# Every third weight slab: the low part made by an accumulating DMA instead of a VectorE subtraction

## The chip, the cores and the metric

The kernel runs on one core of a Trainium2 chip. The metric is device time in microseconds (us), of the whole kernel in one launch; the time of a kernel is the median of its runs. A profiled execution gives the rest: what each engine did at what time. The engines are TensorE (PE; its weight loads are listed as PEld), VectorE (DVE), ScalarE (ACT), GpSimd (POOL) and SyncE (SP, which here only issues DMAs).

## The reference

One layer of a gated recurrent block with an MLP, over 256 frames of width 2048, in float32:

```python
h = RMSNorm(x)
z = h @ w_in + b_in                      # 2048 -> 7 x 2048: xa ya cb cc cx ga gb
xa = rg_lru(causal_dwconv4(xa) + conv_a_b)   # gates by 8 blocks of 256, then a forward scan
out_a = (xa * gelu(ya)) @ w_pa
out_b = (cb * causal_dwconv3(cc * cx)) @ w_pb
x = x + (sigmoid(ga) * out_a + sigmoid(gb) * out_b) @ w_o
x = x + relu(RMSNorm(x) @ w_mlp1)**2 @ w_mlp2    # 2048 -> 8192 -> 2048
return RMSNorm(x)
```

The weights are some 312 MB of float32, each read once.

## The kernel before, in words

Activations lie transposed: features on the 128 partitions, the 256 frames along the free axis. A product is formed for 128 output features at a time, over 2048 input features (16 steps of 128), or 1024 to 4096 in some stages. So that float32 accuracy survives TensorE's faster fp32r format, every operand is split into two fp32r parts: a high part, the value rounded to fp32r, and a low part, the value minus the high part. A step of the product is two matmuls (in `product`, L232 and L233): the high weights times both parts of the activations (512 columns), and the low weights times the high part of the activations (256 columns).

The weights come in slabs of 128 x 1024 float32 (512 KB): 8 steps of one output tile. There are 596 of them, in the order in which TensorE will use them. The class `Weights` streams them. `make` takes the next slab and does three things with it:

- L61: SP issues the DMA that loads the slab into a tile `raw` (4 buffers);
- L63: ScalarE casts `raw` into `hi` (profile name `whi`, 4 buffers);
- L64: VectorE subtracts, `lo = raw - hi` (profile name `wlo`, 4 buffers).

`take` hands TensorE the next slab, after it has let `make` run up to three slabs ahead (`LOOK = 3`). Lines under `high_priority(AHEAD)` are ordered as if they stood 300 instructions earlier in the program, so that the split of a coming slab goes ahead of ScalarE's and VectorE's other work. A planner puts the instructions of each engine into one fixed order and inserts the waits: a buffer is filled again once its last reader is done, and each engine, as well as each queue of DMA issues, works in order. The first four slabs are made by two calls with `parts=4`, a quarter slab at a time, interleaved with the loads of x.

Beside the splits, ScalarE takes the second half of each product out of PSUM (`added`, L238; six PSUM buffers `psz`) and does the activations; VectorE adds, scales, convolves and scans. POOL does nothing but a few memsets: the zero edges of the convolution inputs `xa` (L289) and `cx` (L308), twice each in each of the eight groups of the first stage, which lasts to about 500 us. The stages follow one another in program order: eight groups of the input projection with convolutions, gates and scan; then per output tile the two merge gates and the projections of both branches; the product with `w_o`; and two halves of the MLP.

Of the kernel before, what the change touches and what calls it, by code (L numbers as in the profile page):

```python
# [9 lines left out]
F32 = mybir.dt.float32  # L10
F32R = mybir.dt.float32r
AF = mybir.ActivationFunctionType
ALU = mybir.AluOpType

P = 128
S = 256
# [6 lines left out]
EPS = 1e-6  # L23
LOOK = 3
AHEAD = 300
# [11 lines left out]


class Weights:
    """Streams [128, ncol] slabs of weights and splits each exactly into two fp32r parts."""  # L40

    def __init__(self, tc, raw_pool, hi_pool, lo_pool, slabs):
        self.tc, self.nc, self.slabs = tc, tc.nc, slabs
# [2 lines left out]
        self.at = 0  # L46

    def make(self, n=1, parts=1, before=None):
        """Loads and splits the next n slabs, in that many parts; before(i) precedes part i."""
        nc = self.nc  # L50
        w = HALF * P // parts
        got = [(self.slabs[len(self.made) + m],
                self.raw_pool.tile([P, HALF * P], F32, name="raw"),
                self.hi_pool.tile([P, HALF * P], F32R, name="whi"),
                self.lo_pool.tile([P, HALF * P], F32R, name="wlo")) for m in range(n)]
        for i in range(parts):
            c = slice(i * w, (i + 1) * w)
            if before is not None:
                before(i)
            for src, raw, hi, lo in got:  # L60
                nc.sync.dma_start(raw[:, c], src[:, c])  # L61
                with self.tc.high_priority(AHEAD):
                    nc.scalar.copy(hi[:, c], raw[:, c])  # L63
                    nc.vector.tensor_tensor(lo[:, c], raw[:, c], hi[:, c].bitcast(F32), ALU.subtract)  # L64
        self.made += [(hi, lo) for _, _, hi, lo in got]
# [3 lines left out]
            self.make()  # L69

    def first(self, n):
        """The first n slabs, which make() has made."""
        self.at = n
        return self.made[:n]

# [9 lines left out]
def trunk(ctx: ExitStack, tc: tile.TileContext, xT, par, w_in, w_lru, w_pa, w_pb, w_o, w_1, w_2, out):  # L85
    nc = tc.nc
# [9 lines left out]
    slabs = []  # L96
# [28 lines left out]
    x = keep.tile([P, NT, S], F32, name="x")  # L125
# [3 lines left out]
        return pr[:, OFF[name] + j:OFF[name] + j + 1]  # L129

    def split(dst, src):
        """dst [P, 2, S] fp32r <- src as two parts."""
        nc.scalar.copy(dst[:, 0, :], src)  # L133
        nc.vector.tensor_tensor(dst[:, 1, :], src, dst[:, 0, :].bitcast(F32), ALU.subtract)  # L134

# [12 lines left out]
    ssq = keep.tile([P, S], F32, name="ssq")  # L148

    def total(parts):  # L150
        """PSUM [P, S]: the sum over partitions and parts, on every partition."""
        ps = psl.tile([P, 512], F32, name="psl")
        for i, sq in enumerate(parts):
            nc.tensor.matmul(ps[:, :S], ones, sq, start=i == 0, stop=i == len(parts) - 1)  # L154
        return ps[:, :S]

    def rsqrt(dst, parts):
        """dst [P, S] <- 1 / sqrt(mean of the squares + EPS)."""
        ps = total(parts)
        y = wk.tile([P, S], F32, name="t")  # L160
        nc.scalar.activation(y, ps, AF.Sqrt, scale=1.0 / D, bias=eps)
        m = wk.tile([P, S], F32, name="low")
        nc.vector.tensor_scalar(m, ps, 1.0 / D, EPS, ALU.mult, ALU.add)
        nc.vector.reciprocal(y, y)
        nc.vector.tensor_tensor(m, m, y, ALU.mult)
        nc.vector.scalar_tensor_tensor(m, m, -0.5, y, ALU.mult, ALU.mult)
        nc.vector.scalar_tensor_tensor(dst, m, 1.5, y, ALU.add, ALU.mult)
# [14 lines left out]
    nc.sync.dma_start(pr[:, NT:], par[:, NT:])  # L182

    def squares(src, j):
        """ssq, by partition, of the tiles up to j."""
        if j == 0:
            nc.scalar.activation(ssq, src, AF.Square)
        else:
            sq = wk.tile([P, S], F32, name="s")
            nc.scalar.activation(sq, src, AF.Square)  # L190
            nc.vector.tensor_tensor(ssq, ssq, sq, ALU.add)

    lam = pr[:, OFF["lam"]:OFF["lam"] + NT]
    s4 = keep.tile([P, NT], F32, name="s4")
# [2 lines left out]
    s2 = keep.tile([P, NT], F32, name="s2")  # L197

    def decay():
        """s4 <- -4 softplus(-lam)."""  # L200
        nc.scalar.activation(s2, lam, AF.Abs)
        nc.scalar.activation(sg, s2, AF.Sigmoid, scale=-1.0)
        nc.vector.tensor_scalar(sd, sg, -1.0, 2.0, ALU.mult, ALU.add)
        nc.vector.reciprocal(sd, sd)
        nc.vector.tensor_tensor(sg, sg, sd, ALU.mult)
        nc.vector.tensor_tensor(s2, sg, sg, ALU.mult)
        nc.vector.tensor_scalar(sd, s2, 1.0 / 17, 1.0 / 15, ALU.mult, ALU.add)
        for n in (13, 11, 9, 7, 5, 3, 1):
            nc.vector.tensor_tensor(sd, sd, s2, ALU.mult)
            nc.vector.tensor_scalar(sd, sd, 1.0 / n, None, ALU.add)  # L210
        nc.vector.tensor_tensor(sd, sd, sg, ALU.mult)
        nc.vector.tensor_scalar(s2, lam, -1.0, 0.0, ALU.mult, ALU.max)
        nc.vector.scalar_tensor_tensor(s2, sd, 2.0, s2, ALU.mult, ALU.add)
        nc.vector.tensor_scalar(s4, s2, -4.0, None, ALU.mult)

    def product(acts, k0, nh, flat=False):
        """PSUM [P, 2, S]: the sum of its two halves, or if flat its first half, is the next weights' product
        with acts."""
        ps = psz.tile([P, 2, S], F32, name="psz")
        n = nh * HALF  # L220
        for c in range(nh):
            hi, lo = W.take()
            for k in range(HALF):
                a = acts(k0 + c * HALF + k)
                i = c * HALF + k
                if flat:
                    w = slice(k * P, (k + 1) * P)
                    nc.tensor.matmul(ps[:, 0, :], hi[:, w], a[:, 0, :], start=i == 0, stop=False)  # L228
                    nc.tensor.matmul(ps[:, 0, :], hi[:, w], a[:, 1, :], start=False, stop=False)  # L229
                    nc.tensor.matmul(ps[:, 0, :], lo[:, w], a[:, 0, :], start=False, stop=i == n - 1)  # L230
                    continue
                nc.tensor.matmul(ps, hi[:, k * P:(k + 1) * P], a, start=i == 0, stop=False)  # L232
                nc.tensor.matmul(ps[:, 1, :], lo[:, k * P:(k + 1) * P], a[:, 0, :], start=False, stop=i == n - 1)  # L233
        return ps
# [13 lines left out]
    def z_product():  # L248
        return product(lambda k: xg[:, k], 0, 2)
# [2 lines left out]
        z_done(z_product(), j, dst, func)  # L252

    def first_pair():
        """The products of the first two tiles, side by side, as x and the weights come in."""
        w = W.first(4)
        two = [psz.tile([P, 2, S], F32, name="psz") for _ in range(2)]
        for k in range(NT):
            for m in range(2):
                hi, lo = w[k // HALF * 2 + m]  # L260
                c = slice(k % HALF * P, (k % HALF + 1) * P)
                nc.tensor.matmul(two[m], hi[:, c], xg[:, k], start=k == 0, stop=False)  # L262
                nc.tensor.matmul(two[m][:, 1, :], lo[:, c], xg[:, k, 0, :], start=False, stop=k == NT - 1)  # L263
        return two
# [16 lines left out]
    with tc.tile_pool(name="w1", bufs=1) as w1:  # L281
        first_norm(w1)
        for g in range(NB):
# [3 lines left out]
            for m in range(2):  # L287
                j = 2 * g + m
# [17 lines left out]
            for m in range(2):  # L306
                j = 2 * g + m
# [9 lines left out]
            if g == 0:  # L317
                decay()
            hi, lo = W.take()
# [13 lines left out]
            r, i = gates  # L333
# [16 lines left out]
            for m in range(2):  # L350
                split(ua[:, 2 * g + m], v[:, m, :])
# [3 lines left out]
    for j in range(NT):  # L355
        sa = wk.tile([P, S], F32, name="s")
        sb = wk.tile([P, S], F32, name="s")
        z_tile(Z_GA + j, sa, AF.Sigmoid)
        z_tile(Z_GB + j, sb, AF.Sigmoid)
        tb = added(product(lambda k: ub[:, k], 0, 2))  # L360
        nc.vector.tensor_tensor(sb, sb, tb, ALU.mult)
        ta = added(product(lambda k: ua[:, k], 0, 2))
        nc.vector.tensor_tensor(sa, sa, ta, ALU.mult)
        nc.vector.tensor_tensor(sa, sa, sb, ALU.add)
        split(mg[:, j], sa)
# [8 lines left out]
    for h in range(2):  # L374
# [10 lines left out]
        for j in range(NT):  # L385
            flat = h == 1 and j == NT - 1
# [10 lines left out]
    nc.scalar.activation(last, x[:, NT - 1, :], AF.Square)  # L397
    nc.scalar.activation(x[:, NT - 1, :], x[:, NT - 1, :], AF.Copy, scale=pc("gf", NT - 1))
    rsqrt(rs, [ssq, last])
    at = 0  # L400
    for n in (3, 4, 4, 3, 1, 1):
# [4 lines left out]


def _slabs(w):
    """[K, N] -> [N / 128, K / 1024, 128, 1024]: per 128 columns and 1024 rows, one slab with the rows' low
    index on the partitions."""  # L410
    k, n = w.shape
    w = w.reshape(k // (HALF * P), HALF, P, n // P, P)
    return np.ascontiguousarray(w.transpose(3, 0, 2, 1, 4)).reshape(n // P, k // (HALF * P), P, HALF * P)


def _cols(v):
    """[..., n * 128] -> [128, ... * n]."""
    return np.asarray(v).reshape(-1, P).T


# [28 lines left out]
```

## Time and profile before

| | |
|---|---|
| median of 3 runs (lowest to highest) | 1670.57 us (1669.35 to 1670.81) |
| profiled execution, span from first to last instruction | 1667.7 us |
| the profiled execution's own time | its span; the runs' median is 2.9 us above it |
| TensorE busy | 1645.6 us (99%) |
| VectorE busy | 1124.6 us (67%) |
| ScalarE busy | 866.4 us (52%) |
| POOL busy | 3.4 us |
| mean share of the DMA engines, weight loads | 56.5% |
| subtraction L64, one slab | 1.23 us |
| rounding L63, one slab | 1.05 us |

Busy times of different engines overlap and don't add up. A group of instructions in the profile is named by its line, engine, operation and tiles, "out<-in"; after the bar stand its busy time, the mean duration of one in ns, and the idle time of its engine just before it with what ended that idle time. "ACT whi L63 <- PE psz L232" in the list of waits reads: ScalarE, about to do L63, waited for TensorE's L232; then total, number and longest of these waits.

### The profile page before, as it was taken

To read this page: it belongs to the slowest core of one execution; us is meant where nothing else is said; L and a number is where in the kernel's file an instruction comes from. 1 tells how busy PE (TensorE), PEld (TensorE's weight loads), DVE (VectorE), ACT (ScalarE), POOL (GpSimd) and SP (SyncE) were. 2 spreads that over 40 slices of the span, in tenths; PEclk is the share of its full clock that TensorE was granted. 3 is DMA by queue.
4 is the path that set the end of the run, shared out by engine and by line. 5 is a ranking of instruction groups with operands and counts; after the bars stand their busy time and mean duration, and the time that the engine had idled before them with its cause. 6 is when DMAs were issued, how large, how long until landed. Compare 5 with 4: busy or idle time off the path is not lost.

```text
span 1667.7 us, 24308 instructions
## 1 busy us (share of the span) xinstructions
PE 1645.6 (99%) x9450; PEld 1437.3 (86%) x9450; DVE 1124.6 (67%) x1617; ACT 866.4 (52%) x1270; POOL 3.4 (0%) x37
## 2 busy tenths in 40 slices
PE   8999999999999999999999999999999999999996
PEld 6888888888888888888888888888888888888886
DVE  7989778878977665656666666665555666655554
ACT  7666666666665444444445544444443444444442
POOL 0000000000000000000000000000000000000000
PEclk9999999999999999999999999999999999999998
DMA  7555555555556555555555555555555555555552
GB/s 256 177 191 188 189 190 189 186 189 189 185 186 191 189 189 188 185 188 188 188 189 189 179 189 189 190 190 189 187 188 185 188 189 188 189 190 190 188 188 93
DMA packets 88244, 312.15 MB, mean 187 GB/s; under 512 B 9920, under 2 KB 12352, under 8 KB 88128
## 3 DMA queue, kind: packets, MB, share of 16 engines
q1 hardware_dynamic: 87840, 309.93, 56.5%
q8 instruction: 74, 1.21, 0.3%
q10 hardware_dynamic: 288, 0.66, 0.1%
q14 instruction: 42, 0.34, 0.1%
HBM read 308.45 MB, written 2.10 MB: 186 GB/s over the span
## 4 chain that ended last, share of the span: by engine, by line
PE 97%; DVE 1%; DMA 1%; ACT 0%; issue 0%; SPq 0%; DVEq 0%; ACTq 0%
PE psz L232 62%; PE psz L233 32%; DMA raw<-w_in_s 1%; PE psz L262 1%; PE psl L327 0%; PE psl L328 0%; PE psl L326 0%; DVE wlo L64 0%; PE psz L263 0%; PE psz L229 0%; PE psz L230 0%; PE psz L228 0%; DVE x L403 0%; ACT whi L63 0%; PE psl L154 0%
## 5 line engine op out<-in xcount | busy, mean ns | idle before, releaser
L232 PE MATMUL psz<-big,whi 128*128 128x512 f32 x4048 | 1420.9, 394 | 1.0 <-ACT whi L63 0.8
L233 PE MATMUL psz<-big,wlo 128*128 128x256 f32 x4048 | 1130.5, 279 | 0.8 <-DVE wlo L64 0.8
L64 DVE TENSOR_TENSOR wlo<-raw,whi 128x1024 fp32r<-128x1024 f32 (+1 forms) x596 | 714.0, 1201 | 511.7 <-ACT whi L63 510.6
L63 ACT CAST whi<-raw 128x1024 fp32r<-128x1024 f32 (+1 forms) x596 | 614.3, 1032 | 772.5 <-issue 433.5
L232 PEld LDWEIGHTS psz<-big,whi 128*128 128x128 f32 x4048 | 759.2, 188 | 182.8 <-ACT whi L63 1.1
L233 PEld LDWEIGHTS psz<-big,wlo 128*128 128x128 f32 x4048 | 759.3, 188 | 1.1 <-DVE wlo L64 1.1
L232 PE MATMUL psz<-mg,whi 128*128 128x512 f32 x496 | 174.6, 395 | 0.0
L233 PE MATMUL psz<-mg,wlo 128*128 128x256 f32 x496 | 139.0, 281 | 0.0
L232 PEld LDWEIGHTS psz<-mg,whi 128*128 128x128 f32 x496 | 93.0, 187 | 22.1 <-DVE mg L134 0.3
L240 DVE TENSOR_TENSOR t<-psz,low 128x256 f32<-128x256 f32 x255 | 105.7, 417 | 0.0
L233 PEld LDWEIGHTS psz<-mg,wlo 128*128 128x128 f32 x496 | 93.7, 189 | 0.0
L238 ACT COPY low<-psz 128x256 f32<-128x256 f32 x255 | 93.1, 365 | 0.0
L245 DVE TENSOR_TENSOR t<-t,rs 128x256 f32<-128x256 f32 x112 | 47.1, 422 | 2.3
L380 DVE SCALAR_TENSOR_TENSOR s<-t 128x256 f32<-128x256 f32 x64 | 27.2, 425 | 2.1
L338 DVE RECIPROCAL q<-q 128x512 f32<-128x512 f32 x8 | 26.8, 3346 | 0.0
L294 DVE SCALAR_TENSOR_TENSOR xc<-xa,pr,xc 128x256 f32<-128x256 f32 x48 | 22.0, 475 | 0.0
L134 DVE TENSOR_TENSOR big<-s,big 128x256 fp32r<-128x256 f32 x48 | 20.1, 419 | 0.0
L262 PE MATMUL psz<-big,whi 128*128 128x512 f32 x32 | 14.0, 478 | 5.7 <-ACT whi L63 5.7
L133 ACT CAST big<-s 128x256 fp32r<-128x256 f32 x48 | 19.3, 402 | 0.0
L327 PE MATMUL psl<-xs,whi 128*128 128x256 f32 x64 | 18.0, 281 | 0.0
L328 PE MATMUL psl<-xs,wlo 128*128 128x256 f32 x64 | 17.9, 280 | 0.0
L326 PE MATMUL psl<-xs,whi 128*128 128x256 f32 x64 | 17.8, 278 | 0.0
(122 smaller groups left out, 529.4 us busy)
## 6 DMA issues: line engine op xcount, KB each, us to landing
raw<-w_s SPq DMA_DIRECT2D x256, 512.0 KB, 3.5
raw<-w_in_s SPq DMA_DIRECT2D x220, 512.0 KB, 4.2
raw<-w_pb_s SPq DMA_DIRECT2D x32, 512.0 KB, 4.2
raw<-w_pa_s SPq DMA_DIRECT2D x32, 512.0 KB, 4.1
raw<-w_o_s SPq DMA_DIRECT2D x32, 512.0 KB, 3.5
raw<-w_lru_s SPq DMA_DIRECT2D x8, 512.0 KB, 4.0
x<-xT SPq DMA_DIRECT2D x8, 256.0 KB, 4.4
raw<-w_in_s SPq DMA_DIRECT2D x16, 128.0 KB, 4.2
```

The lines of the kernel that those rows point to most:

```text
L63: nc.scalar.copy(hi[:, c], raw[:, c])
L64: nc.vector.tensor_tensor(lo[:, c], raw[:, c], hi[:, c].bitcast(F32), ALU.subtract)
L134: nc.vector.tensor_tensor(dst[:, 1, :], src, dst[:, 0, :].bitcast(F32), ALU.subtract)
L232: nc.tensor.matmul(ps, hi[:, k * P:(k + 1) * P], a, start=i == 0, stop=False)
L233: nc.tensor.matmul(ps[:, 1, :], lo[:, k * P:(k + 1) * P], a[:, 0, :], start=False, stop=i == n - 1)
L238: nc.scalar.copy(low, ps[:, 1, :])
L240: nc.vector.tensor_tensor(t, ps[:, 0, :], low, ALU.add)
L245: nc.vector.tensor_tensor(t, t, rs, ALU.mult)
L262: nc.tensor.matmul(two[m], hi[:, c], xg[:, k], start=k == 0, stop=False)
L294: nc.vector.scalar_tensor_tensor(c, xa[:, m, tap:tap + S], pc("ca_w", tap * NT + j), c, ALU.mult, ALU.add)
L338: nc.vector.reciprocal(q, q)
L380: nc.vector.scalar_tensor_tensor(v, t, 0.0, t, ALU.max, ALU.mult)
```

## The change

For slabs made in one piece whose index leaves 2 when divided by 3 (5, 8, 11 and so on), VectorE's subtraction is left out. ScalarE casts `raw` into `hi` as before, writes a second, negated copy of `raw` into `lo`, rounded to fp32r in the same way (so `lo` holds minus `hi`), and GpSimd issues a DMA that adds `raw` onto `lo` in place. `lo` then holds `raw - hi`. The other slabs are split as before. Docstrings are removed as well.

```diff
             for src, raw, hi, lo in got:
                 nc.sync.dma_start(raw[:, c], src[:, c])
+                if parts == 1 and len(self.made) % 3 == 2:
+
+                    with self.tc.high_priority(AHEAD):
+                        nc.scalar.copy(hi, raw)
+                        nc.scalar.activation(lo, raw, AF.Copy, scale=-1.0)
+                        nc.gpsimd.dma_start(lo.bitcast(F32), raw, accum_op=ALU.add)
+                    continue
                 with self.tc.high_priority(AHEAD):
                     nc.scalar.copy(hi[:, c], raw[:, c])
                     nc.vector.tensor_tensor(lo[:, c], raw[:, c], hi[:, c].bitcast(F32), ALU.subtract)
```

## The prediction

> **What bounds the kernel now.** I read the page from the top: busy shares, slices, the DMA queues, the chain of work that ended last, the costliest groups.
>
> ```profile
> span 1667.7 us, 24308 instructions
> PE 1645.6 (99%) x9450; PEld 1437.3 (86%) x9450; DVE 1124.6 (67%) x1617; ACT 866.4 (52%) x1270; POOL 3.4 (0%) x37
> ...
> PEclk9999999999999999999999999999999999999998
> DMA  7555555555556555555555555555555555555552
> ...
> q1 hardware_dynamic: 87840, 309.93, 56.5%
> ...
> PE 97%; DVE 1%; DMA 1%; ACT 0%; issue 0%; SPq 0%; DVEq 0%; ACTq 0%
> ...
> L232 PE MATMUL psz<-big,whi 128*128 128x512 f32 x4048 | 1420.9, 394 | 1.0 <-ACT whi L63 0.8
> L233 PE MATMUL psz<-big,wlo 128*128 128x256 f32 x4048 | 1130.5, 279 | 0.8 <-DVE wlo L64 0.8
> L64 DVE TENSOR_TENSOR wlo<-raw,whi 128x1024 fp32r<-128x1024 f32 (+1 forms) x596 | 714.0, 1201 | 511.7 <-ACT whi L63 510.6
> L63 ACT CAST whi<-raw 128x1024 fp32r<-128x1024 f32 (+1 forms) x596 | 614.3, 1032 | 772.5 <-issue 433.5
> ```
>
> TensorE is busy 99% of the span and is 97% of the chain. The subtraction (L64) is VectorE's largest group, 714.0 us, but the idle time that it causes in front of L233 is 0.8 us in all. The waits say the same, and name who stands behind whom:
>
> ```profile
> ACT whi L63 <- PE psz L232: 317.1, 212, 1.9
> POOL cx L308 <- DVE cc L314: 236.5, 7, 35.0
> POOL xa L289 <- DVE xc L294: 140.8, 6, 23.5
> ...
> PE psz L262 <- ACT whi L63: 5.7, 2, 5.1
> ...
> PE psz L232 <- ACT whi L63: 0.8, 1, 0.8
> PE psz L233 <- DVE wlo L64: 0.8, 1, 0.8
> ```
>
> The first row is the clue to this kernel's rhythm: the rounding on ScalarE waits for TensorE to give a buffer back, not the other way round. The windows show where TensorE is idle at all: 7.9 us of the first 42, nothing in a window of the steady part.
>
> ```profile
> 0.00:42.00 42.00, 34.10 (x161) 28.37 (x162) 29.79 (x62) 31.21 (x58) 0.54 (x9) 0.96 0.79 255
> ...
> 250.00:500.00 250.00, 250.00 (x1463) 219.48 (x1462) 209.41 (x320) 160.84 (x247) 1.47 (x14) 1.00 0.57 187
> ```
>
> (Columns: window, its length, busy PE, PEld, DVE, ACT, POOL, granted clock, DMA share, GB/s.) The clock is at 1.00 there, so a stall of TensorE has no throttled clock to win back from.
>
> **The slack of one slab.** Two stretches of the timeline, one of ScalarE and one of all engines:
>
> ```profile
> 199.61 1.05 ACT L63 CAST whi<-raw 128x1024 fp32r<-128x1024 f32 x1 [1.18 <-PE psz L232]
> 202.41 1.06 ACT L63 CAST whi<-raw 128x1024 fp32r<-128x1024 f32 x1 [1.75 <-PE psz L232]
> ```
>
> ```profile
> 799.50 1.05 ACT L63 CAST whi<-raw 128x1024 fp32r<-128x1024 f32 x1 [1.75 <-PE psz L232]
> 799.73 0.39 PE L232 MATMUL psz<-big,whi 128*128 128x512 f32 x1
> 799.96 0.28 PE L233 MATMUL psz<-big,wlo 128*128 128x256 f32 x1
> ...
> 800.58 1.23 DVE L64 TENSOR_TENSOR wlo<-raw,whi 128x1024 fp32r<-128x1024 f32 x1 [1.57 <-ACT whi L63]
> ...
> 801.83 0.33 SPq L61 DMA_DIRECT2D raw<-w_pa_s  x1
> ```
>
> TensorE eats a slab in 202.41 - 199.61 = 2.80 us. The rounding of slab t+4 starts the moment slab t is done (four buffers each of high and low parts), and TensorE wants the low part of t+4 three slabs later, 0.23 us into that slab (799.73 to 799.96): 3 x 2.80 + 0.23 = 8.63 us from the buffer's release. Today the low part is ready at 800.58 + 1.23 = 801.81, 2.31 us after the release: 6.3 us to spare. The load that reuses the raw buffer goes out at 801.83, right behind it.
>
> **The change part by part.** The rule picks slabs 5, 8, ... 593: 197 of 596.
>
> VectorE loses 197 x 1.23 = 242 us of work. On the path that is worth at most the 0.8 us of waits above; I take nothing.
>
> ScalarE gains 197 passes over 1024 columns. The trace has no scaled pass of that width; its rows are these:
>
> ```profile
> L63 ACT CAST whi<-raw 128x1024 fp32r<-128x1024 f32 x580 | 608.6, 1049 | 771.2 <-issue 433.5 <-PE psz L232 317.1 <-ACT low L238 15.9
> ...
> L137 ACT ACTIVATE big<-x,pr 128x256 fp32r<-128x256 f32 x32 | 15.4, 504 | 2.5 <-DMA pr<-par 1.6 <-DMA x<-xT 0.9
> ...
> L271 ACT ACTIVATE gate<-x,pr 128x512 f32<-128x512 f32 x2 | 1.4, 717 | 0.0
> ```
>
> From 256 to 512 columns an activation grows by 0.213 us; two more such steps make 0.717 + 0.43 = 1.14 us, against 1.05 for the cast. I take 1.14. In all 225 us, hidden by ScalarE's idle half (at its fullest, in the window from 250 to 500 us, it works 160.84 of 250 us; 0.14 more per us of time, 1.14 in 8.40, still fits). Behind the pass wait the evictions and bias activations of ScalarE, 1.14 us later than before; PSUM has six buffers for them, so nothing. On the accumulated slab's own path, the low part's negative is ready 1.05 + 1.14 = 2.19 us after the release, and 8.63 - 2.19 = 6.44 us are left for the DMA.
>
> The DMA is issued by POOL, waits for ScalarE, reads two operands and writes one; TensorE and SP wait for its landing. No row shows an accumulating DMA. The nearest are the weight loads, of the same 512 KB:
>
> ```profile
> raw<-w_s SPq DMA_DIRECT2D x256, 512.0 KB, 3.5
> raw<-w_in_s SPq DMA_DIRECT2D x220, 512.0 KB, 4.2
> ```
>
> The load queue takes 56.5% of 1667.7 us = 942 us for 309.93 MB, so 0.524 MB take 1.59 us of the 16 engines; of the 3.5 us to landing 1.9 us are fixed. From below, the accumulation costs one plain transfer undisturbed: 3.5 us, 2.9 to spare, and no stall. From above it costs three passes (two reads and a write that don't overlap, 4.78 us), every packet alternating with one of a load (4.78 more), and 1.9: 11.5 us, 5.0 us too late. I take two passes, 3.19 us, since reads and writes of a copy overlap already in the loads' price and only the second read is new. And I take full alternation with loads, 3.19 more, for this reason: the raw buffer now comes free at the landing instead of 2.3 us after the release, SP's queue is in order, so the load that waits for that buffer holds back the two behind it, whose buffers are long free. The three go out together, 4.78 us of transfers, just when the next accumulation, one slab cycle of 8.40 us later, starts. So 1.9 + 3.19 + 3.19 = 8.28 us, 1.84 us more than there is.
>
> How much of it TensorE feels: from the release by slab t to the use of slab t+4 there lies also slab t+1, which is accumulated too and stalls as well. Two stalls in a row together make up 1.84 us, so each is 0.92 us: 197 x 0.92 = 181 us. The DMA engines carry it (3 x 1.59 + 3.19 = 7.97 us in each 9.3).
>
> The Trainium skill has a rule on the size of the second read: "Collectives: The Full Stack", in its part on the bandwidth ceiling, says that a reducing transfer runs at half the rate of a copy because it reads two sources. No run here shows that yet; by it the transfer is the two passes taken above.
>
> **The edges.** At the start (first window: ACT 31.21 of 42, DMA share 0.79, TensorE waiting 5.7 us for ScalarE) slabs 5, 8 and 11 add three passes to an engine that TensorE waits for: between 0 and 3 x 1.14 = 3.4 us; I take 2. The end is untouched: slabs 594 and 595 are of the old kind. Sum: 1667.7 + 181 + 2 = 1850.7 us of span; the runs' median, 1670.57, lies 2.9 us above the profiled span: **1853.6 us**.
>
> **The rivals.**
> 1. *Not slower.* The accumulation lands within 6.44 us of its issue, most simply because it costs as one transfer (3.5 us by the load's row) and the loads don't bunch. Then low parts are in time, VectorE's relief is off the path, and the time is 1670.6 to 1673 us. For it: 43% of the DMA engines' time is free. Against: the added read and the bunched loads. The point that decides is 6.44 us. The Trainium skill, "DMA: Bandwidth & Descriptors", section on the anatomy of a DMA on the gpsimd path, gives 2.0 us plus the bytes at 436 GB/s, an estimate of 3.2 us for these bytes; it fits a plain transfer, and by it the result would be this rival's.
> 2. *The DMA engines become the bound.* With three passes the load and accumulation take 9.56 us of each 8.40: at least 1.16 us per accumulated slab, 229 us, so 1900; with the full lateness of 5.02 us, half of it each time, 197 x 2.51 = 494 us, so 2165 us. For it: nothing in the trace says that an add at a DMA engine goes at a copy's rate.
> 3. *POOL's queue.* Today POOL's memsets stand up to 35.0 us at the head of its queue, waiting for VectorE (rows above, 13 such waits). A DMA queued behind one is late by what is left of it. If each of 13 such memsets costs 5 us of stall in the first 490 us: 65 us, so 1736 us. Against: the DMAs carry a priority 300 instructions ahead, so they should stand in front.
>
> **How the numbers follow.** My forecast, two passes and bunched loads, with half its stall and one and a half times it as its own range (1760 to 1945 us): 0.45. Rival 1: 0.20. Rival 2: 0.25. Rival 3: 0.08. Left: 0.02 that the relief of VectorE and of the first 42 us brings over 0.2%. A measurement of this kernel tells about 0.2%, 3.3 us, from no change: of rival 1, 0.18 is within that and 0.02 slower. So faster 0.02, same 0.18, slower 0.80. The range reaches from rival 1, 1668 us, to the end of rival 2, 2165 us; above it lie adds at a third of the copy rate or less.
>
> **What would show it.** After the change: VectorE near 883 us, ScalarE near 1090; idle time before L233 some 180 us, released by a DMA into wlo, on about 197 matmuls, 0.9 us each; the accumulation's issue to landing 8 us; loads going out in threes; DMA share 0.8 or more in the steady slices; no stall at the other 399 slabs. The prediction is wrong if the landing comes within 6.4 us (rival 1), if the DMA share stands at 0.9 and more and the stalls are over 2 us (rival 2), or if TensorE's waits gather around POOL's memsets (rival 3).

## The result and the profile after

The changed kernel takes 1699.5 us (median of 3 runs, 1692.96 to 1700.75) against 1670.57 us: a ratio of 1.0169, 95% interval 1.0155 to 1.0183. It is slower, by 29 us where 183 were forecast. Where the runs of one kernel fell into a faster and a slower state, times below are medians of the fast ones. The page after:

```profile
span 1697.7 us, 25140 instructions
PE 1655.0 (97%) x9450; PEld 1439.2 (85%) x9450; DVE 908.9 (54%) x1424; ACT 1045.1 (62%) x1463; POOL 169.2 (10%) x230
...
DMA  8788888888888888888888888888888888888884
...
q1 hardware_dynamic: 87840, 309.93, 52.5%
q0 software_dynamic: 27792, 101.20, 31.8%
...
PE 80%; DMA 11%; issue 4%; ACT 2%; DVE 2%; SPq 0%; DVEq 0%; POOLq 0%; POOL 0%; ACTq 0%
...
L240 PE MATMUL psz<-big,wlo 128*128 128x256 f32 x4048 | 1135.4, 281 | 22.2 <-DMA wlo<-raw 21.0
...
L240 PEld LDWEIGHTS psz<-big,wlo 128*128 128x128 f32 x4048 | 760.8, 188 | 30.9 <-DMA wlo<-raw 28.9
...
L66 ACT ACTIVATE wlo<-raw 128x1024 fp32r<-128x1024 f32 x193 | 203.4, 1054 | 0.0
...
wlo<-raw POOLq DMA_DIRECT2D x193, 512.0 KB, 4.9
```

VectorE is relieved by 216 us and ScalarE loaded by 179, where 242 and 225 had been worked out. The accumulations take 31.8% of the DMA engines' time. But TensorE waits for them 21.0 us in all, not 181: the median accumulation lands 4.9 us after its issue, inside the 6.44 us that were left for it. The waits of TensorE and of SP's queue after:

```profile
PE psz L240 <- DMA wlo<-raw: 21.0, 18, 2.6
```

```profile
SPq L61 <- DMA wlo<-raw: 486.4, 192, 9.9
```

By the matmuls' rows 18 of 193 accumulations are late; the weight loads (PEld), which wait first, count 28.9 us. Of the 30 us between the two profiled spans some 20 are idle time of TensorE; the other 9.4 are busy time (1655.0 after 1645.6). Part of these is the clock: its record in the trace stands at half for 3.41 us three times (from 58.7, 96.3 and 1267.1 us, each within 1.2 us of the end of a wait of 2.0 us or more), before the change once, which makes 2 x 1.7 = 3.4 us. The remaining 6 us are not resolved.

Where the loss arises is shown by the first and last starts of two groups of matmuls (the gates of the first stage, and the `w_o` and MLP products on the tile `mg`), before and then after:

```profile
L233 PE MATMUL psz<-mg,wlo x496: 277/280/285, 844.4 to 1635.2; 128*128 128x256 f32 x166
...
L328 PE MATMUL psl<-xs,wlo x64: 280/280/280, 70.9 to 485.1; 128*128 128x256 f32 x64
```

```profile
L335 PE MATMUL psl<-xs,wlo x64: 278/280/281, 76.2 to 505.5; 128*128 128x256 f32 x64
...
L240 PE MATMUL psz<-mg,wlo x496: 277/280/285, 864.9 to 1665.1; 128*128 128x256 f32 x166
```

The loss is 5.3 us by the first gates, 20.4 by the end of the first stage, 20.5 at 844 us, 29.9 at the end: two thirds of it fall in the first 485 us, none in the next 360.

What sets half of the late accumulations (9 of 18) apart from those on time is what SP's queue did just before. Three loads of a cycle on time, then of a late one, with POOL's issue and the matmul that waited (start, duration, engine):

```profile
853.10 3.13 SPq L61 DMA_DIRECT2D raw<-w_o_s  x3
```

```profile
858.67 0.86 POOL L67 DMA_DIRECT2D wlo<-raw  x1 [7.54 <-ACT wlo L66]
```

```profile
327.60 1.28 SPq L61 DMA_DIRECT2D raw<-w_in_s  x3
```

```profile
329.79 0.86 POOL L67 DMA_DIRECT2D wlo<-raw  x1 [0.93 <-ACT low L245]
```

```profile
337.82 0.39 PE L240 MATMUL psz<-big,wlo 128*128 128x256 f32 x1 [1.52 <-DMA wlo<-raw]
```

On time, the loads go out over 3.13 us, ending 2.4 us ahead of the accumulation. Late, the three go out within 1.28 us, ending 0.9 us ahead of it. One group of the first stage further the same row stands again, 61.8 us later (389.37, three loads in 1.28 us; the accumulation at 391.99; TensorE waits 2.47 us at 400.80).

The difference lies in the fixed order of SP's queue. In each cycle one of the three loads asks for the raw buffer of an accumulated slab, and the queue stands still in front of that load until the accumulation has landed. After 171 of the 192 landings it is the second of the three: the first is out already (853.10), and the other two follow the landing at 854.94. In 18 cases it is the first, and all three leave at once: the accumulation in the row below lands at 327.55 us, and SP, which has waited 8.6 us for it, sends at 327.60.

```profile
321.36 0.86 POOL L67 DMA_DIRECT2D wlo<-raw  x1 [7.78 <-ACT big L140]
```

Behind those 18 landings 9 accumulations are late, behind all others 9 as well.

I took the packets of both queues from the trace (us; medians, in the last line means):

```
                                        all 193   the late one at 329.79
ScalarE's negated copy to POOL's issue     0.29                     0.30
issue to first packet                      1.44                     3.56
first packet's start to last one's end     3.10                     4.17
load packets under way between the two       29                      156
one 4 KB row: accumulation 0.347, load 0.187
```

In 142 of the 193 the first packet goes out within 1.5 us of the issue; in ten it takes over 3, and the load packets run first. The delay follows the backlog of loads: with fewer than 20 load rows issued but not begun 1.1 us after POOL's issue, the first packet comes after 1.43 us in the median (127 cases), with over 200 after 3.84 us (9 cases). VectorE's work in the same time shows no such tie (correlation 0.16 against 0.88 for the backlog).

### The profile page after: what moved, and what is told of

The parts are those of the page before. It is cut to its first block, busy times and chain, and to the rows that moved or that the text cites. A ratio compares the mean times of both kernels' runs of the same rounds, so it can differ in the third digit from the quotient of the medians.

```text
span 1697.7 us, 25140 instructions
## 1 busy us (share of the span) xinstructions
PE 1655.0 (97%) x9450; PEld 1439.2 (85%) x9450; DVE 908.9 (54%) x1424; ACT 1045.1 (62%) x1463; POOL 169.2 (10%) x230
## 3 DMA queue, kind: packets, MB, share of 16 engines
q0 software_dynamic: 27792, 101.20, 31.8%
## 4 chain that ended last, share of the span: by engine, by line
PE 80%; DMA 11%; issue 4%; ACT 2%; DVE 2%; SPq 0%; DVEq 0%; POOLq 0%; POOL 0%; ACTq 0%
PE psz L239 52%; PE psz L240 27%; DMA wlo<-raw 7%; DMA raw<-w_in_s 2%; DMA raw<-w_s 1%; DVE wlo L71 1%; ACT whi L70 1%; DMA x<-xT 0%; ACT whi L65 0%; ACT wlo L66 0%; ACT gate L338 0%; PE psl L333 0%; PE psl L334 0%; PE psl L335 0%; DMA raw<-w_pb_s 0%
## 5 line engine op out<-in xcount | busy, mean ns | idle before, releaser
L240 PEld LDWEIGHTS psz<-big,wlo 128*128 128x128 f32 x4048 | 760.8, 188 | 30.9 <-DMA wlo<-raw 28.9
L71 DVE TENSOR_TENSOR wlo<-raw,whi 128x1024 fp32r<-128x1024 f32 (+1 forms) x403 | 479.7, 1192 | 506.4 <-ACT whi L70 503.7
L70 ACT CAST whi<-raw 128x1024 fp32r<-128x1024 f32 (+1 forms) x403 | 411.5, 1023 | 370.3 <-PE psz L239 154.1
L65 ACT CAST whi<-raw 128x1024 fp32r<-128x1024 f32 x193 | 202.4, 1049 | 254.3 <-issue 146.9
L67 POOL DMA_DIRECT2D wlo<-raw x193 | 166.8, 864 | 1436.7 <-ACT wlo L66 579.1
L66 ACT ACTIVATE wlo<-raw 128x1024 fp32r<-128x1024 f32 x193 | 203.4, 1054 | 0.0
L141 DVE TENSOR_TENSOR big<-s,big 128x256 fp32r<-128x256 f32 x48 | 20.2, 422 | 34.2 <-ACT big L140 34.2
L145 DVE SCALAR_TENSOR_TENSOR big<-x,pr,big 128x256 fp32r<-128x256 f32 x32 | 14.7, 481 | 16.8 <-ACT big L144 16.7
L141 DVE TENSOR_TENSOR mg<-s,mg 128x256 fp32r<-128x256 f32 x32 | 13.5, 421 | 17.2 <-ACT mg L140 17.2
```

Source lines behind the costliest of these rows:

```text
L65: nc.scalar.copy(hi, raw)
L66: nc.scalar.activation(lo, raw, AF.Copy, scale=-1.0)
L67: nc.gpsimd.dma_start(lo.bitcast(F32), raw, accum_op=ALU.add)
```

## The experiments

Theory A: the accumulations that land late are the cost, all others are free, and they are late because loads leave SP's queue in a bunch shortly ahead of them. Rivals: B, ScalarE's extra passes; C, the sum of the DMA traffic; D, POOL's queue or issue; and, whatever the cause, a price that every accumulation pays alike. Ratios are to the kernel before.

**ScalarE's pass alone**

```diff
-                        nc.gpsimd.dma_start(lo.bitcast(F32), raw, accum_op=ALU.add)
+                        nc.vector.tensor_tensor(lo, raw, hi.bitcast(F32), ALU.subtract)
```

> ScalarE still writes the negated copy for every third slab, but VectorE then subtracts over it as before and no DMA adds anything. Theory A (the loss of 29 us comes from accumulating DMAs that land too late for TensorE, 18 waits on them in the profile): TensorE waits for no low part outside the start, 1670 to 1675 us. Theory B (ScalarE's extra 193 passes cost it, by delaying roundings and evictions): 1695 to 1705 us.

1668.74 us, 0.9994 (0.9985 to 1.0004). With ScalarE at 1049.5 us of work nothing is lost, so rival B falls, and so do the 2 us that the prediction put on these passes at the start.

**Accumulations only behind, or only in, the first stage**

```diff
-                if parts == 1 and len(self.made) % 3 == 2:
+                if parts == 1 and len(self.made) % 3 == 2 and len(self.made) >= 172:   # or < 172
```

> Accumulations only from slab 172 on, behind the eight groups: 137 of the 193. Theory A: only the handful of waits seen after 1000 us is left, 9 to 10 us, so about 1680 us. Theory B, or any price that every accumulation pays alike: 137/193 of 29 us, so about 1691 us.

> Accumulations only in the first stage, slabs 5 to 170: 56 of the 193. Theory A (the first stage's slabs meet a late ScalarE and POOL's memsets): about 20 us, so 1690 us. A price that every accumulation pays alike: 56/193 of 29 us, so 1679 us.

1675.03 us, 1.0033 (1.0023 to 1.0042), for the 137 late ones; 1687.23 us, 1.0111 (1.0092 to 1.0130), for the 56 early ones. The 56 cost three times as much as the 137: the price is not alike. Nor does it follow the sum of the traffic (rival C), as the 137 move 2.4 times the bytes. Each came out some 3 to 5 us under what theory A gave it.

**The negated copy ahead of the rounding**

```diff
-                        nc.scalar.copy(hi, raw)
                         nc.scalar.activation(lo, raw, AF.Copy, scale=-1.0)
                         nc.gpsimd.dma_start(lo.bitcast(F32), raw, accum_op=ALU.add)
+                        nc.scalar.copy(hi, raw)
```

> ScalarE writes the negated copy first, POOL issues the DMA, and the rounding into the high part comes after it. Each accumulation starts 1.05 us earlier, with the same work everywhere. Theory A: of 21.0 us of waits for accumulations 6.4 us are left when 1.05 us is taken from each of the 18, and the knock-on loss goes with them: 1676 to 1686 us. Theory B: the same work on ScalarE, no change, 1699 us. Rival C (the DMA engines' total load delays the weight loads): no change, 1699 us.

1721.53 us, 1.0310 (1.0295 to 1.0325). The expectation missed, and the run is no test of it: the planner puts ScalarE's instructions in its own order, and in 183 of the 193 cases the rounding still stands first. The ten others, one to each group of the first stage among them, made that stage end 26.6 us later than in the changed kernel (gates at 529.4 against 502.8). It shows how sensitive that stage is to order, and no more.

**Five raw buffers**

```diff
-    rawp = ctx.enter_context(tc.tile_pool(name="rawp", bufs=4))
+    rawp = ctx.enter_context(tc.tile_pool(name="rawp", bufs=5))
-    wk = ctx.enter_context(tc.tile_pool(name="wk", bufs=3))
+    wk = ctx.enter_context(tc.tile_pool(name="wk", bufs=2))
```

> Five raw buffers instead of four (and two instead of three buffers each for the small work tiles, to make room). A load then no longer waits for the landing of the accumulation just before it. Theory A (late accumulations are those that meet loads which were held back and go out in a bunch): loads go out singly, SP's 486 us of waits for accumulations mostly vanish, the pairs of late accumulations end, 1675 to 1690 us. Theory C (the DMA engines' total load, 84% of their time, is the cost): the same bytes, 1699 us.

The control, the kernel before with the same two lines:

> The kernel before, with five raw buffers and two instead of three of the small work tiles: the control of the two runs with five raw buffers. All theories: TensorE is busy throughout either way, 1667 to 1673 us.

1691.82 us, 1.0143 (1.0114 to 1.0171); the control 1667.21 us, 0.9988 (0.9978 to 0.9997). SP's waits for accumulations did not vanish (471.8 us after 486.4): SP runs ahead until something blocks it, and with one more buffer that is still the accumulation. The expectation missed. In the first stage this kernel loses as much as before, 20.2 us to its control, and 16 landings still release three loads at once. From 844 us on it loses 2 us in the profile, where the changed kernel loses 9.4. That is not shown to be the fifth buffer's doing: with four, the kernel with late accumulations only loses 2.5 us in this stretch, and the one with two places left out (below) 1.8. The accumulations of the stretch are the same in all four, so the late part of the loss does not follow the traffic's sum (rival C) either.

**Two pools of raw buffers**

```diff
-                self.raw_pool.tile([P, HALF * P], F32, name="raw"),
+                (self.acc_pool if parts == 1 and len(self.made) % 3 == 2 else self.raw_pool).tile(...),   # 2 and 3 buffers
```

> Raw buffers as in the run with five (1691.8 us), but in two pools: two for the accumulated slabs, three for the others. The load behind an accumulation then no longer asks for the accumulation's own buffer; the next load that does comes three slabs later. The accumulations, ScalarE's passes and the bytes are the same. Theory A (accumulations are late because loads that were held back for the landing go out together and get ahead of the next accumulation): SP's 472 us of waits for accumulations fall below 150, TensorE's 15 us of waits for them below 6, 1672 to 1681 us. Theory C (the DMA engines' load alone): no change, 1688 to 1695 us.

1692.53 us, 1.0144 (1.0126 to 1.0163): no change against five in one pool. That is the time that rival C was given, and theory A missed by 11 us. But SP's waits for accumulations, which were to go, stand at 479.6 us, and 14 landings still release three loads at once: the hold-back was moved, not ended, so the run does not separate the two.

**A copy in place of the accumulation** (it leaves out the subtraction for these slabs)

```diff
-                        nc.gpsimd.dma_start(lo.bitcast(F32), raw, accum_op=ALU.add)
+                        nc.gpsimd.dma_start(lo.bitcast(F32), raw)
```

> POOL's DMA copies the raw slab over the low part and adds nothing, so the subtraction is left out for these slabs. Same queue, same issues, one read instead of two. Theory A (the length of the accumulation decides how often it is late): a packet takes 0.19 us as a load's does, instead of 0.35, the landing comes after some 3.3 us, TensorE waits less than 5 us for it, 1670 to 1678 us. Theory D (it is POOL's queue or its issue, whatever the DMA does): 1690 us or more.

1673.94 us, 1.0025 (1.0016 to 1.0034). The queue, the landing and the waits:

```profile
q0 software_dynamic: 27792, 101.20, 14.8%
...
wlo<-raw POOLq DMA_DIRECT2D x193, 512.0 KB, 3.1
```

```profile
PE psz L240 <- DMA wlo<-raw: 4.2, 4, 1.4
```

The same bytes on the same queue take half the DMA engines' time without the add (14.8% after 31.8%; a row 0.159 us after 0.347), land 1.8 us earlier, and four are late. POOL's queue as such is not the cost, though its issue is shorter here too, 0.53 us instead of 0.86.

**Every second and every fourth slab**

```diff
-                if parts == 1 and len(self.made) % 3 == 2:
+                if parts == 1 and len(self.made) % 2 == 1:     # or % 4 == 3
```

> Every second slab instead of every third, 290 accumulations. Two loads and an accumulation take 2 x 1.50 + 2.77 = 5.77 us of the DMA engines, and TensorE needs 5.60 us for two slabs. Theory A: the DMA engines become the bound, at least 290 x 0.17 = 50 us and meetings with loads every time, 1740 to 1900 us, DMA share 0.95 or more. A price that every accumulation pays alike (29 us for 193): 1714 us.

> Every fourth slab, 145 accumulations. A longer time from one accumulation to the next (11.2 us) lets the held-back loads run out before it. Theory A: few are late, 1673 to 1684 us. A price that every accumulation pays alike: 145/193 of 29 us, 1692 us.

Every second: 1853.13 us, 1.1099 (1.1042 to 1.1157). Every fourth: 1676.59 us, 1.0046 (1.0030 to 1.0063). The waits of the first:

```profile
DMA  9989989898999999999999999999999999989996
...
q1 hardware_dynamic: 87840, 309.93, 47.7%
q0 software_dynamic: 41760, 152.06, 45.1%
```

```profile
PE psz L240 <- DMA wlo<-raw: 116.9, 96, 3.4
```

290 accumulations cost 183 us, 193 cost 29, 145 cost 7: a step where the DMA engines are nearly full (92.8% for the two queues). That looks like rival 2 of the prediction, the DMA engines as the bound, one step of density further; no run separates it from waits of another cause.

**Two DMAs of half the columns each**

```diff
-                        nc.gpsimd.dma_start(lo.bitcast(F32), raw, accum_op=ALU.add)
+                        for e in (slice(0, 512), slice(512, 1024)):
+                            nc.gpsimd.dma_start(lo[:, e].bitcast(F32), raw[:, e], accum_op=ALU.add)
```

> The accumulation is issued as two DMAs of 512 columns each. TensorE needs the second half 1.4 us after the first. Theory A: the first half lands some 1.4 us earlier, of 21.0 us of waits about 5 are left, 1676 to 1688 us. Theory D (POOL's issue costs): twice the issues, 0.86 us each, 1699 us or more.

1832.23 us, 1.0958 (1.0907 to 1.1009), far from what was expected. A half lands after 7.0 us in the median, TensorE waits 129 times, and the accumulations start at 840.13, 848.21, 859.75, 867.66 and 877.41 us. Over the whole run the cycle of three slabs is 9.2 us in the mean, where the changed kernel has 8.6. That is near the 9.3 that the prediction had worked out for the kernel as changed, but not by its sum: here the second half lands 8.1 us after its issue, and most landings still release only two loads.

**Only the second half by DMA, the first by VectorE**

```diff
+                        a, b = slice(0, 512), slice(512, 1024)
+                        nc.vector.tensor_tensor(lo[:, a], raw[:, a], hi[:, a].bitcast(F32), ALU.subtract)
-                        nc.scalar.activation(lo, raw, AF.Copy, scale=-1.0)
-                        nc.gpsimd.dma_start(lo.bitcast(F32), raw, accum_op=ALU.add)
+                        nc.scalar.activation(lo[:, b], raw[:, b], AF.Copy, scale=-1.0)
+                        nc.gpsimd.dma_start(lo[:, b].bitcast(F32), raw[:, b], accum_op=ALU.add)
```

> For the chosen slabs VectorE subtracts columns 0 to 511 and the accumulating DMA does only columns 512 to 1023: one DMA of half the bytes, whose result TensorE needs 1.4 us later. Theory A: landing about 1.4 us earlier and wanted 1.4 us later, so 2.8 us more to spare; TensorE waits for next to none, 1670 to 1676 us. Theory D (two or more DMAs in flight from POOL are bad in themselves, half rows are slow): 1690 us or more.

1735.5 us (two runs, 1722.77 and 1748.21), 1.0397 (1.0307 to 1.0486), with half the bytes to add and more time to spare. The expectation missed outright, and the profile shows what it had left out. SP's queue, POOL and TensorE in one cycle:

```profile
1411.11 1.28 SPq L61 DMA_DIRECT2D raw<-w_s  x3
```

```profile
1411.98 0.86 POOL L69 DMA_DIRECT2D wlo<-raw  x1 [8.04 <-ACT low L247]
```

```profile
1411.01 0.38 PE L242 MATMUL psz<-big,wlo 128*128 128x256 f32 x1 [0.23 <-DMA wlo<-raw]
```

```profile
SPq L61 <- DMA wlo<-raw: 1356.4, 192, 9.4
```

An accumulation lands at 1411.0: TensorE goes on, and SP sends the three loads that were held back, together. Within the same microsecond the next accumulation is issued, and no packet of it starts before 1417, when the three loads' rows have nearly all gone. In the median of this kernel the first packet comes 4.40 us after the issue, in 142 of 193 cases over 3 us, although the rows then take only 2.55 us. So a DMA of half the bytes lands after 7.1 us, and the loads wait for it again. The cycle is 8.8 us in the mean. It is not the changed kernel's plan in another state: after 188 of its landings SP's order has the wait in front of the first load, so all three are held back together.

**Each accumulation issued 1.05 us later**

```diff
                         nc.scalar.activation(lo, raw, AF.Copy, scale=-1.0)
+                        nc.scalar.activation(lo, raw, AF.Copy, scale=-1.0)
```

> ScalarE writes the negated copy twice, so that each accumulation is issued 1.05 us later; nothing else changes. The median landing would come some 2.4 + 0.3 + 4.9 = 7.6 us after the buffer's release plus 1.05, 8.6 us, at the edge of the 8.63 us that TensorE leaves. Theory A with two states (an accumulation that is late holds back three loads, they go out together and stand in front of the next accumulation, which is late again): most accumulations are late, 0.5 to 1 us each, 1770 to 1870 us, the period of three slabs above 9 us. Theory A without that feedback: 1.05 us more on each of the 18 late ones and a few new ones, 1715 to 1730 us. Theory B (ScalarE's passes): about 1728 us.

1724.01 us, 1.0329 (1.0310 to 1.0347): the second of the three forecasts, without the loop. TensorE waits 40 times, 31.4 us. Rival B gives the same number, but the run of ScalarE's pass alone lost nothing. The first packets here come after 1.43 us in the median, and one alone takes over 3 us: issued later, the accumulations stand clear of the loads. In this kernel's order no landing releases three loads. So lateness alone does not start the loop; that going out together with the held-back loads does is argued from this and the run before.

**Two places of each group left out**

The first stage's groups have 21 slabs, so that every third slab is always the same seven places of a group. Counting slabs from the gates, the late ones of the profile stand mostly at places 5 and 14.

```diff
-                if parts == 1 and len(self.made) % 3 == 2:
+                if parts == 1 and len(self.made) % 3 == 2 and not (
+                        len(self.made) < 168 and len(self.made) % 21 in (5, 14)):
```

> In the eight groups of the first stage (21 slabs each, so that the rule of every third slab picks the same seven places in each group) the slabs at places 5 and 14 are split as before the change: 16 accumulations fewer, 177 of 193. Place 5 is the slab whose accumulation is issued within 2.2 us after three loads that left SP's queue together behind the gates' work; most late ones of the first stage stand at these two places. Theory A: the first stage loses about 8 us instead of 20, 1683 to 1690 us. A price that every accumulation pays alike: 16/193 of 29 us, 1697 us.

> The same with five raw buffers and the smaller work pool, 177 accumulations. With five buffers the profile showed no late accumulation of any size after the first 850 us. Theory A: first stage about 8 us, the rest 2 us, and 2 us less for the small pool's kernel: 1674 to 1682 us. Alike price: 177/193 of 24 us above 1667 us, 1689 us.

1679.03 us, 1.0062 (1.0047 to 1.0078), and with five raw buffers 1676.03 us, 1.0042 (1.0028 to 1.0056). TensorE's waits and the gates' matmuls in the first of them:

```profile
PE psz L240 <- DMA wlo<-raw: 6.7, 7, 1.9
```

```profile
L335 PE MATMUL psl<-xs,wlo x64: 277/280/389, 71.0 to 486.0; 128*128 128x256 f32 x64
```

Sixteen accumulations fewer, one in twelve, take away 20 of the 29 us, and the first stage ends 0.9 us behind the kernel before instead of 20.4. That is more than theory A was given (12 us) and over eight times what an even price would give. Neither version beats the kernel before; the one that does, by 0.12%, is the control with five raw buffers and no accumulation.

## Why the prediction was right and wrong

The direction, the bound and the bookkeeping held. TensorE stayed the bound; VectorE's 216 us brought nothing that shows; ScalarE's passes were hidden (1.054 us each, against 1.14 taken). The early edge was not what it was taken for: 5.3 us are lost by the first gates, to late accumulations, and none to ScalarE's passes, which had 2 us. The count of slabs was off: 596 are instructions of L64, 16 of them quarters, so there are 584 slabs and 193 accumulations, not 197.

The price of the add held. Two passes, 3.19 us, were taken; 8 rows of 0.347 us make 2.78 us, and against the copy on the same queue the add costs 0.347 / 0.159 = 2.2 times. The Trainium skill's rule in "Collectives: The Full Stack", in its part on the bandwidth ceiling, that a reducing transfer runs at half the rate of a copy because it reads two sources, agrees with both. The Trainium skill's formula in "DMA: Bandwidth & Descriptors", section on the anatomy of a DMA on the gpsimd path, gives 3.2 us for these bytes: the copy landed after 3.1, the accumulation after 4.9. So it gives the copy's landing and not the accumulation's. Rival 1 came close to true in spite of the add: 170 of the 193 landed within its 6.44 us.

The step that failed is the third term of the landing, "full alternation with loads, 3.19 more", taken for every accumulation. Without it the sum gives 1.9 + 3.19 = 5.09 us, and 4.9 came out, not 8.28; in the median only 29 load packets of 384 run beside an accumulation. The reason that the prediction gave for the term does not hold: I had assumed that the load that waits for the landing stands in front of two others, and that the three go out just when the next accumulation starts. After 171 of 192 landings only two loads go out, and they are out 2.4 us before the next issue. The assumption was circular as well: the loads come just in front of the next accumulation if the last one landed late, and it lands late if they do. Such lateness is passed on (below), but in the changed kernel it dies out after a cycle or two.

What is left of the forecast mechanism is the 18 landings that do release three loads, and I had not asked where the cycle is irregular. From the second group of the first stage on they come at the same two places of a group, 2 and 11, because SP's order is fixed there in that way, and the accumulations that follow, at places 5 and 14, are 9 of the 12 that come late in this stage. Why the planner orders these two places otherwise stays open.

Later, from 1000 us on, the few late ones come in pairs. Beside the accumulations of 1257.57, 1328.60 and 1464.77 us a load's row took 1.56, 1.44 and 2.48 us (0.187 is the mean); they began on time and ended late, and the next one found the loads in front of it. That the slow row is the cause is not shown: one of 1.59 us at 1053.86 us made no accumulation late. What makes a single row so slow, and why POOL began one issue at 996.67 us 2 us late, stays open; so does why the halves are late so often when a delay of 1.05 us costs so little.

Rival 3, POOL's memsets, fell: POOL's issue begins 0.3 us after ScalarE's pass in all but three of the 193 cases. The memsets stand in the queue, but behind the accumulations' turns.

## What to carry to other kernels

A transfer that fits its slack on its own tells little; ask what is issued in the two microseconds ahead of it, whether its own landing releases that, and which of the queue's entries stands still for it: here three loads behind the wait instead of two made the difference. Before multiplying a stall by a count, look whether the on-time case sustains itself too, and then look for the places where the cycle is irregular: here 16 of 193 slabs carried 20 of 29 us. Moving work off an engine that TensorE doesn't wait for brought nothing here, and a DMA engine share of 84% leaves little room for disorder.

## What the runs showed of the hardware

- An accumulating DMA between tiles takes 0.347 us in the mean for a 4 KB row, a copy on the same queue 0.159 us, a load from HBM 0.187 us. POOL's issue is 0.86 us for the one and 0.53 us for the other.
- A transfer issued on POOL's queue just after, or even in the same microsecond as, loads on SP's queue started its first packet 3 to 5 us after the issue (1.44 us otherwise), and in the time beyond 1.44 us 98 to 200 load packets began. The Trainium skill, "DMA: Bandwidth & Descriptors", section on queues, rings and completion order, has a DMA engine go round the queues packet by packet; the trace agrees where the last rows of both queues went out one by one (one row of each queue in turn, about 0.48 us a pair, from 1264 to 1265.4 us), and shows no such turns at these starts; whether the accumulation's packets stood in their queue by then, it does not tell.
- The same bytes in two DMAs, or half the bytes in one, made the kernel slower, 1.0958 and 1.0397 times the kernel before against 1.0169: when a transfer starts mattered more than how long it is.
- The granted clock fell to half for 3.41 us just after three of the longest waits of TensorE for an accumulation (2.58, 2.04 and 1.98 us), at 58.7, 96.3 and 1267.1 us; after another, of 2.47 us at 400.8 us, it did not.
